# Prompt tokens in even-first order in a two-layer decoder step: dilated attention groups computed among tokens of one parity

## The chip, the cores and the metric

The kernel runs on one core of one Trainium2 chip. The metric is the time of one execution in microseconds of the device (us). Everything is computed in one launch.

## The reference, cut to what matters

Two layers process 256 prompt tokens and 8 x 4 sampled tokens together (model width 1024). The input projection w_in gives queries, keys and values for 12 heads of 64, in three groups of 4 heads, and two gate parts. A prompt query in group g looks at the keys at distances 0, d, 2d, ... up to its window:

```python
DIL_PATTERNS = ((128, 1), (512, 4), (2048, 16))     # (window, dilation) of the groups
dist = dilation * jnp.arange(window // dilation + 1)
...
idx = rows[:, None] - dist[None, :]
valid = idx >= 0
kg = jnp.take(k_all, idx, axis=1)
s = jnp.einsum('bqhd,bqjhd->bqhj', qc, kg).astype(jnp.float32) * scale
s = jnp.where(valid[None, :, None, :], s, NEG)
m = jnp.max(s, -1, keepdims=True)
pr = jnp.exp(s - m)
o = jnp.einsum('bqhj,bqjhd->bqhd', pr, vg.astype(jnp.float32)) / den[..., None]
...
mixw = jax.nn.softmax(jnp.stack(lses, 0), axis=0)   # over the three groups
```

Since the groups are weighted by their denominators, one softmax over the keys of all three groups gives the same. In groups 1 and 2 the distances are multiples of 4 and of 16, so an even query never meets an odd key. The sampled tokens attend to caches of 128, 512 and 1024 positions and to their own few new rows. Beside the attention a gate multiplies u with a causal 128 x 128 product of normalised gate rows (the spatial weights). Then follow the mixer's output projection, a cross attention to 256 memory tokens, and a feed-forward part, each with a residual and a normalisation. Outputs are also the new keys and values.

## The kernel before, in words

Activations lie with features on the partitions and the 288 tokens as columns. A linear layer is done for 128 outputs at a time: for each of 8 k-tiles three matmuls (high part by high weight, low by high, high by low, L361 to L363) of 288 columns. SP loads weights in blocks of 256 columns (`wraw`, three buffers, L148); ACT and DVE split each block half by half into a high part `wh` (L343) and a low part `wl` (L344).

The attention of a layer lies inside and behind the projection w_in, which has 22 blocks of 128 outputs, 528 matmuls. `Tasks` (L170) is a planner: every piece of attention work is a generator that yields costs; while w_in is written out, pieces whose time has come are put between its matmuls, by priority, and what is left is written out behind it (`drain`). Then a scheduler orders each engine's list by a model of the times. On the chip each engine takes its list in order. The pieces are:

- `prompt_all` and `prompt_scores(p)`, p = 0, 1 (L891): for each group g and each half h2 of a pair of heads, scores in a PSUM bank `tr` (three buffers), L902 (128 later queries by 256 keys) and L906 (128 earlier queries by 128 keys), on 64 rows of the array; DVE adds the mask and takes the maximum (L910, custom instruction and a read of the accumulator); exp on ACT (L919); normalisation on DVE (L929); transposes on PE (L933, L935), copied to `pt` by ACT (L939).
- `prompt_pv(p)` (L943): value products L952 and L955, evicted by ACT (L957) and DVE (L958). These are only possible behind w_in, since their targets `attH`, `attL` are set up there.
- `decode_scores`: the caches' keys come in blocks `cu` (128 x 1024, five buffers, and three lent ones, `cv`), are multiplied with the queries on POOL (L1059) or DVE (L1061), and are summed up on DVE (L1062). `query(g)` turns a group's queries by PE (L1041), ACT copies them (L1043), and they go out to DRAM (L1045) and come back spread over the partitions (L1048 on SP's queue). The sums times a constant give `zs` (L1068), which PE adds up (L1074). After the softmax PE transposes the weights `dp` (L1096 to L1109).
- `decode_pv` (L1117): value products of the caches, L1128, 4 matmuls on 32 columns of the array for each block; then the new rows (L1138), a copy (L1141, L1142), transposes (L1149) and copies `at` (L1158, L1160). A cache block's buffer is free when its products are done; only then SP loads the next block into it. The last blocks are group 2's: two halves of 64 partitions for each buffer.
- `natural` (L798): keys and values turned to token order for the outputs (L804, L811); `gate_norm`, `spatial_weights` (L748) and `sgu` (L865; L872, L877): the gate.

SP's list holds all the loads in one order, so a load that waits for a buffer holds up every load behind it. Behind the attention SP also loads the memory's tokens, `mem_nat` (L1195).

## Time and profile before

| what | value |
|---|---|
| three runs | 1072.79, 1073.74, 1076.74 us, median 1073.74 |
| profiled execution | 1073.84 us, its span 1072.1 us |
| PE busy | 1026.8 us, 96% of the span |
| DVE, ACT, POOL busy | 763.2 (71%), 531.0 (50%), 189.2 us (18%) |
| DMA | 213.68 MB, 199 GB/s on average |

The profile shows one execution; its 1.7 us outside the span are start and end of the program. The stages are read from the trace: attention of layer 0 to about 142 us, then mixer, cross attention and feed-forward to 560, attention of layer 1 to 672, and the rest. Busy times of engines overlap. A PE row's length holds the time that a matmul takes through the array; matmuls follow one another faster than that, so the step from one start to the next is the cost.

### The profile page before, as it was taken

How to read it: one execution, taken by the hardware profiler on the slowest of the kernel's cores; microseconds unless marked ns; L12 is line 12 of the kernel's file. 1: busy time of each engine (PE TensorE's matmuls, PEld its weight loads, DVE VectorE, ACT ScalarE, POOL GpSimd, SP SyncE). 2: the span in 40 equal slices, each digit the busy share in tenths (PEclk: the TensorE clock that was granted, in tenths of full speed). 3: DMA queues.
4: the chain of work that ended last, by engine and by line, in shares of the span. 5: the costliest groups of instructions: out<-in, count | busy, mean ns of one | idle time of the engine just before them, and what ended most of it. 6: DMA issues, size and time to landing. Idle time of an engine off the chain costs nothing. (4 is left out here: it accounts for less than half of the span.)

```text
span 1072.1 us, 20130 instructions
## 1 busy us (share of the span) xinstructions
PE 1026.8 (96%) x8038; PEld 958.7 (89%) x8038; DVE 763.2 (71%) x1406; ACT 531.0 (50%) x1000; POOL 189.2 (18%) x151
## 2 busy tenths in 40 slices
PE   8999999999999999999988999999999999999995
PEld 7989589988799999999977985998888999999994
DVE  6698679855489756565996876897464996565656
ACT  4427546543458535353562364565353685354431
POOL 5592013000023000000448500220000410000000
PEclk8999999999999999999999999999999999999997
DMA  9999844777944555544455898447874465545431
GB/s 290 299 260 316 243 166 154 245 267 255 325 129 143 190 169 181 158 158 161 155 162 165 241 302 235 141 161 237 285 277 157 142 177 165 185 163 191 165 117 44
DMA packets 185533, 213.68 MB, mean 199 GB/s; under 512 B 5760, under 2 KB 175136, under 8 KB 185440
## 3 DMA queue, kind: packets, MB, share of 16 engines
q1 hardware_dynamic: 177216, 205.00, 60.1%
q10 hardware_dynamic: 8224, 7.41, 2.1%
q8 instruction: 63, 1.03, 0.4%
q14 instruction: 30, 0.25, 0.1%
HBM read 203.80 MB, written 8.59 MB: 198 GB/s over the span
## 5 line engine op out<-in xcount | busy, mean ns | idle before, releaser
L343 ACT ACTIVATE wh<-wraw 128x1024 fp32r<-128x1024 f32 (+1 forms) x237 | 249.3, 1054 | 285.6 <-PE acc L362 234.2
L344 DVE TENSOR_TENSOR wl<-wraw,wh 128x1024 fp32r<-128x1024 f32 (+1 forms) x237 | 308.4, 1304 | 100.1 <-ACT wh L343 99.5
L361 PE MATMUL acc<-xH,wh 128*128 128x288 f32 x728 | 219.0, 301 | 3.2 <-DVE fy L533 3.2
L363 PE MATMUL acc<-xH,wl 128*128 128x288 f32 x728 | 217.3, 299 | 2.7 <-DVE wl L344 2.7
L362 PE MATMUL acc<-xL,wh 128*128 128x288 f32 x728 | 218.5, 301 | 1.2 <-DVE xL L640 1.2
L361 PE MATMUL acc<-hH,wh 128*128 128x288 f32 x512 | 151.1, 295 | 0.0
L362 PE MATMUL acc<-hL,wh 128*128 128x288 f32 x512 | 151.1, 295 | 0.0
L363 PE MATMUL acc<-hH,wl 128*128 128x288 f32 x512 | 150.8, 295 | 0.0
L361 PEld LDWEIGHTS acc<-xH,wh 128*128 128x128 f32 x728 | 139.5, 192 | 4.4 <-issue 2.5
L363 PEld LDWEIGHTS acc<-xH,wl 128*128 128x128 f32 x728 | 138.9, 191 | 4.0 <-DVE wl L344 3.6
L362 PEld LDWEIGHTS acc<-xL,wh 128*128 128x128 f32 x728 | 139.1, 191 | 2.3 <-DVE xL L640 1.9
L551 POOL TENSOR_TENSOR s<-s,xres 128x288 f32<-128x288 f32 x15 | 20.2, 1349 | 444.8 <-DVE s L547 444.1
L361 PEld LDWEIGHTS acc<-hH,wh 128*128 128x128 f32 x512 | 96.4, 188 | 0.0
L362 PEld LDWEIGHTS acc<-hL,wh 128*128 128x128 f32 x512 | 96.4, 188 | 0.0
L363 PEld LDWEIGHTS acc<-hH,wl 128*128 128x128 f32 x512 | 96.2, 188 | 0.0
L361 PE MATMUL acc<-fH,wh 128*128 128x290 f32 x256 | 78.3, 306 | 1.8 <-DVE fy L533 1.8
L362 PE MATMUL acc<-fL,wh 128*128 128x290 f32 x256 | 76.9, 301 | 0.2 <-DVE fL L525 0.2
L363 PE MATMUL acc<-fH,wl 128*128 128x290 f32 x256 | 75.8, 299 | 0.5 <-DVE wl L344 0.5
L361 PEld LDWEIGHTS acc<-fH,wh 128*128 128x128 f32 x256 | 48.3, 189 | 2.6 <-PE acc L363 2.2
L362 PEld LDWEIGHTS acc<-fL,wh 128*128 128x128 f32 x256 | 48.5, 190 | 1.2 <-DVE fL L525 0.6
L363 PEld LDWEIGHTS acc<-fH,wl 128*128 128x128 f32 x256 | 48.1, 189 | 1.2 <-DVE wl L344 1.0
L1059 POOL TENSOR_TENSOR cu<-cu,qb 128x1024 f32<-128x1024 f32 x15 | 43.5, 2917 | 13.1 <-DMA qb<-qd 9.6
(326 smaller groups left out, 2182.2 us busy)
## 6 DMA issues: line engine op xcount, KB each, us to landing
cu<-cache_mem_kv SPq DMA_DIRECT2D x64, 512.0 KB, 7.4
wraw<-w_up SPq DMA_DIRECT2D x32, 1024.0 KB, 5.5
wraw<-w_down SPq DMA_DIRECT2D x32, 1024.0 KB, 4.8
wraw<-w_in SPq DMA_DIRECT2D x21, 1024.0 KB, 5.7
cu<-cache_kv_w SPq DMA_DIRECT2D x42, 512.0 KB, 8.5
wraw<-w_xkv SPq DMA_DIRECT2D x16, 1024.0 KB, 6.4
wraw<-w_mix_out SPq DMA_DIRECT2D x8, 1024.0 KB, 10.1
wraw<-w_xq SPq DMA_DIRECT2D x8, 1024.0 KB, 4.9
```

The lines of the kernel that those rows point to most:

```text
L343: S.activation(h[:, r], raw[:, r], AF.Copy)
L344: gates[f"split{k}"] = behind(V.tensor_sub(lo[:, r], raw[:, r], h[:, r].bitcast(F32)), "dve")
L361: m = T.matmul(ps, wh[:, k], H[:, k], start=first, stop=False)
L362: T.matmul(ps, wh[:, k], L[:, k], start=False, stop=False)
L363: T.matmul(ps, wl[:, k], H[:, k], start=False, stop=last)
L551: eng.tensor_add(self.s, self.s, xres[:, n])
L1059: G.tensor_mul(cu, cu, qb[g])
```

## The change

The 256 prompt tokens lie in another order: in each half of 128, first the 64 even ones, then the 64 odd ones. The order is made where the tokens are read (a load of two neighbouring tokens to a partition, and transposes that write to the two places); rotary tables, masks, the gate's spatial weights and all outputs are adapted to it (three more output DMAs on ACT's queue in a layer). Group 0 is computed as before. In groups 1 and 2 the scores are taken only among tokens of one parity, on 64 x 64 pieces of the array: the half of rows is h2, the half of columns is the parity h. Their two results share one bank and one set of columns (gg = 1), so masks, exp, normalisation and transposes run over 768 columns for each half instead of 1152. The value products of groups 1 and 2 take 64 columns each. The planner's costs are the same 700 for a step of scores (two steps for each p now, not three), 700 instead of 1000 for a half's transposes, and 650 for each group's value products. Lines move: L902/L906 are L935 (both) for group 0, and L946, L949, L953 for the others; L933/L935 become L982; L952/L955 become L997/L1000 and L1011; L1041 becomes L1098, L1061 L1118, L1062 L1119, L1068 L1125, L1074 L1131, L1096 L1153, L1109 L1166, L1128 L1185, L148 L156, L344 L352, L361 to L363 L369 to L371, L1195 L1252.

```diff
-    dist = 128 + np.arange(128)[:, None] - np.arange(256)[None, :]
-    for g, (win, dil) in enumerate(((128, 1), (512, 4), (2048, 16))):
+    row = np.arange(128)
+    tok = 2 * (row % 64) + row // 64
+    dist = 128 + tok[:, None] - np.concatenate([tok, 128 + tok])[None, :]
+    c[:, C_MQ:C_MQ + 256] = np.where((dist >= 0) & (dist <= 128), 0.0, NEG)
+    for g, (win, dil) in ((1, (512, 4)), (2, (2048, 16))):
+        jj, b = row // 64, row % 64
+        j = jj if g == 1 else 1 - jj
+        key = (128 * j + 2 * b)[None, :] + (row // 64)[:, None]
+        dist = 128 + tok[:, None] - key
         ok = (dist >= 0) & (dist <= win) & (dist % dil == 0)
-        c[:, C_MQ + 256 * g:C_MQ + 256 * (g + 1)] = np.where(ok, 0.0, NEG)
+        c[:, C_MQ + 128 + 128 * g:C_MQ + 256 + 128 * g] = np.where(ok, 0.0, NEG)
...
-        nc.sync.dma_start(out=x_nat[:, :, h], in_=I["x_prompt"][0, :, h].rearrange("(a p) d -> p a d", p=128))
+        nc.sync.dma_start(out=x_nat[:, :, h], in_=I["x_prompt"][0, :, h].rearrange("(p a) d -> p a d", p=128))
...
-            T.transpose(ps[:, 128 * a:128 * a + 128], x_nat[:, a, 128 * n:128 * n + 128], ident)
+            T.transpose(ps[:, 0:256].rearrange("p (j q b) -> p q j b", j=2, q=2)[:, a],
+                        x_nat[:, a, 128 * n:128 * n + 128], ident)
...
-            G.affine_select(out=wm, in_=wm, pattern=[[0, 4], [-1, 128]], compare_op=ALU.is_ge,
-                            fill=0.0, base=0, channel_multiplier=1)
+            wsp = stg("wsp")
+            for q in range(2):
+                G.affine_select(out=wsp.rearrange("p (g q b) -> p q g b", g=4, q=2)[:, q],
+                                in_=wm.rearrange("p g (b q) -> p q g b", q=2)[:, q],
+                                pattern=[[0, 4], [-2, 64]], compare_op=ALU.is_ge, fill=0.0, base=-q,
+                                channel_multiplier=1)
...
-                S.copy(vt[g, a], ps)
+                if g:
+                    src = ps[:, 0:256].rearrange("p (j h c) -> p h j c", j=2, h=2)
+                    S.copy(vt[g, a][:, 0:256].rearrange("p (h j c) -> p h j c", h=2, j=2),
+                           src if g == 1 else src[:, :, ::-1])
+                    S.copy(vt[g, a][:, 256:288], ps[:, 256:288])
+                else:
+                    S.copy(vt[g, a], ps)
...
         def prompt_scores(p):
-            pt = slot([128, 2, 3, 384], name="pt")
+            pt = slot([128, 2, 2, 384], name="pt")
             att[f"pt{p}"] = pt
             sc, ms = [], []
             for h2 in range(2):
-                sc.append(ptile(1152).rearrange("p (g k) -> p g k", g=3))
+                sc.append(ptile(1152)[:, 0:768])
                 ms.append(small(12, "m"))
-            for g in range(3):
+            for gg in range(2):
                 b = [tr(), tr()]
+                if gg == 0:
+                    for q, c, d in (((128, 256), (0, 256), (0, 256)), ((0, 128), (0, 128), (256, 384))):
+                        for h2 in range(2):
+                            r = slice(64 * h2, 64 * h2 + 64)
+                            T.matmul(b[h2][:, d[0]:d[1]], qT[r, p, q[0]:q[1]], kT[r, p, c[0]:c[1]],
+                                     start=True, stop=True)
+                else:
+                    for g in (1, 2):
+                        n = 2 * g + p
+                        for i in (1, 0):
+                            for h2 in range(2):
+                                for h in range(2):
+                                    r, o = slice(64 * h2, 64 * h2 + 64), slice(64 * h, 64 * h + 64)
+                                    keys = kT[r, n, 0:256].rearrange("p (j c) -> p j c", j=2)[:, :, o]
+                                    if i == 0:
+                                        T.matmul(b[h2][o, 192 + 64 * g:256 + 64 * g], qT[r, n, o], keys[:, 0],
+                                                 start=True, stop=True, skip_group_check=True)
+                                    elif g == 1:
+                                        T.matmul(b[h2][o, 0:128], qT[r, n, 128 + 64 * h:192 + 64 * h], keys,
+                                                 start=True, stop=True, skip_group_check=True)
+                                    else:
+                                        for j in range(2):
+                                            T.matmul(b[h2][o, 192 - 64 * j:256 - 64 * j],
+                                                     qT[r, n, 128 + 64 * h:192 + 64 * h], keys[:, j],
+                                                     start=True, stop=True, skip_group_check=True)
                 for h2 in range(2):
-                    r = slice(64 * h2, 64 * h2 + 64)
-                    T.matmul(b[h2][:, 0:256], qT[r, 2 * g + p, 128:256], kT[r, 2 * g + p, 0:256],
-                             start=True, stop=True)
-                for h2 in range(2):
-                    r = slice(64 * h2, 64 * h2 + 64)
-                    T.matmul(b[h2][:, 256:384], qT[r, 2 * g + p, 0:128], kT[r, 2 * g + p, 0:128],
-                             start=True, stop=True)
-                for h2 in range(2):
-                    for i, (k0, k1, c) in enumerate(((0, 256, 0), (256, 384, 128))):
-                        V.tensor_tensor_reduce(out=sc[h2][:, g, k0:k1], in0=b[h2][:, k0:k1], in1=mq[:, g, c:256],
-                                               scale=1.0, scalar=-3e38, op0=ALU.add, op1=ALU.max,
-                                               accum_out=ms[h2][:, 3 * i + g:3 * i + g + 1])
+                    for i, (k0, k1) in enumerate(((0, 256), (256, 384))):
+                        d = 512 * i + (128, 256)[1 - i] * gg
+                        c = (256 * gg, (128, 320)[gg])[i]
+                        V.tensor_tensor_reduce(out=sc[h2][:, d:d + k1 - k0], in0=b[h2][:, k0:k1],
+                                               in1=mq[:, c:c + k1 - k0], scale=1.0, scalar=-3e38,
+                                               op0=ALU.add, op1=ALU.max,
+                                               accum_out=ms[h2][:, 2 * i + gg:2 * i + gg + 1])
...
-                for g in range(3):
+                for gg in range(2):
                     ps = tr()
-                    T.transpose(ps[:, 0:128], s[:, g, 256:384], ident)
-                    for k in range(2):
-                        T.transpose(ps[:, 128 + 128 * k:256 + 128 * k], s[:, g, 128 * k:128 * k + 128], ident)
-                    if g in PT_DVE:
-                        V.tensor_copy(pt[:, h2, g], ps[:, 0:384])
-                    else:
-                        S.copy(pt[:, h2, g], ps[:, 0:384])
-                yield 1000, 0
+                    for n, c in enumerate(((512, 0, 128), (640, 256, 384))[gg]):
+                        T.transpose(ps[:, 128 * n:128 * n + 128], s[:, c:c + 128], ident)
+                    S.copy(pt[:, h2, gg], ps[:, 0:384])
+                yield 700, 0
...
         def prompt_pv(p):
             H, L, pt = att["H"], att["L"], att.pop(f"pt{p}")
-            for g in range(3):
-                ps = acc()
-                for tt in range(2):
-                    for h2 in range(2):
-                        c = 256 * g + 64 * (2 * p + h2)
-                        o = ps[64 * h2:64 * h2 + 64]
-                        if tt == 0:
-                            T.matmul(o[:, 0:256], vn[:, c:c + 64], pt[:, h2, g, 0:256],
-                                     start=True, stop=False, skip_group_check=True)
-                        else:
-                            T.matmul(o[:, 128:256], vn[:, 768 + c:768 + c + 64], pt[:, h2, g, 256:384],
-                                     start=False, stop=True, skip_group_check=True)
-                S.activation(H[:, 2 * g + p, 0:256], ps[:, 0:256], AF.Copy)
-                V.tensor_sub(L[:, 2 * g + p, 0:256], ps[:, 0:256], H[:, 2 * g + p, 0:256].bitcast(F32))
-                yield 650, 0
+            for gs in ((0,), (1, 2)):
+                ps = {g: acc() for g in gs}
+                if 0 in ps:
+                    for tt in range(2):
+                        for h2 in range(2):
+                            c = 64 * (2 * p + h2)
+                            o = ps[0][64 * h2:64 * h2 + 64]
+                            if tt == 0:
+                                T.matmul(o[:, 0:256], vn[:, c:c + 64], pt[:, h2, 0, 0:256],
+                                         start=True, stop=False, skip_group_check=True)
+                            else:
+                                T.matmul(o[:, 128:256], vn[:, 768 + c:768 + c + 64], pt[:, h2, 0, 256:384],
+                                         start=False, stop=True, skip_group_check=True)
+                else:
+                    for i in (1, 0):
+                        for h in range(2):
+                            for g in gs:
+                                for h2 in range(2):
+                                    c = 768 * h + 256 * g + 64 * (2 * p + h2)
+                                    o = ps[g][64 * h2:64 * h2 + 64, 128 * i + 64 * h:128 * i + 64 * h + 64]
+                                    r = slice(0, 128) if i else slice(64 * g - 64, 64 * g)
+                                    k0 = 128 * g * i + 64 * h
+                                    T.matmul(o, vn[r, c:c + 64], pt[r, h2, 1, k0:k0 + 64],
+                                             start=True, stop=True, skip_group_check=True)
+                for g in gs:
+                    S.activation(H[:, 2 * g + p, 0:256], ps[g][:, 0:256], AF.Copy)
+                    V.tensor_sub(L[:, 2 * g + p, 0:256], ps[g][:, 0:256], H[:, 2 * g + p, 0:256].bitcast(F32))
+                yield 650 * len(gs), 0
```

PE in layer 0, where w_in ends. Before: its last matmul (L363), then scores of p = 1, the transposes of the sampled tokens' weights `dp`, value products, and the first cache products (`o<-cu`).

```order
L363 MATMUL acc<-xH,wl 128x288
L902 MATMUL tr<-kT,qT 128x256
L906 MATMUL tr<-kT,qT 128x128
L1096 MATMUL tr<-const,dp 128x128 x2
L1097 MATMUL tr<-const,s_1192 128x128
L1109 MATMUL tr<-const,dp 32x128 x3
L952 MATMUL acc<-pt,vn 64x256 x2
L955 MATMUL acc<-pt,vn 64x128 x2
L902 MATMUL tr<-kT,qT 128x256
L906 MATMUL tr<-kT,qT 128x128
L1128 MATMUL o_1287<-cu,z_87 32x256 x8
L1128 MATMUL o_1287<-cu,zp_89 32x256 x4
```

Now the last scores of p = 1 and the first `dp` transposes stand 34 matmuls of w_in ahead of its end:

```order
L370 MATMUL acc<-xL,wh 128x288
L949 MATMUL tr<-kT,qT 64x128 x2
L946 MATMUL tr<-kT,qT 64x64 x2
L953 MATMUL tr<-kT,qT 64x64 x2
L949 MATMUL tr<-kT,qT 64x128 x2
L946 MATMUL tr<-kT,qT 64x64 x2
L953 MATMUL tr<-kT,qT 64x64 x6
L946 MATMUL tr<-kT,qT 64x64 x4
L1153 MATMUL tr<-const,dp 128x128 x2
L1154 MATMUL tr<-const,s_1229 128x128
L371 MATMUL acc<-xH,wl 128x288
```

And at w_in's end (L371 is its last matmul) the second cache products follow at once; the first four stand nine matmuls ahead of them:

```order
L371 MATMUL acc<-xH,wl 128x288
L1185 MATMUL o_1357<-cu,z_87 32x256 x4
L997 MATMUL acc<-pt,vn 64x256 x2
L1000 MATMUL acc<-pt,vn 64x128 x2
L1185 MATMUL o_1357<-cu,zp_89 32x256 x8
L1185 MATMUL o_1357<-cv,zp_89 32x256 x12
```

No scores are left behind w_in. In the same way the scale products L1131 stand earlier in w_in: 8 of them with 144 of its matmuls still to come in layer 0 (before 116; in layer 1 144 both times), and the next 4 with 87 to come in layer 1 (before 44). Layer 1's transposes of group 2's query (L1098) stand later: 146 to come, before 207.

DVE in layer 1, ahead of group 2's `zs`. Before, its products (L1061) and reduces (L1062) stand between splits of weights:

```order
L344 TENSOR_TENSOR wl<-wraw,wh 128x1024
L1062 TENSOR_REDUCE st<-cu 128x16 x2
L916 TENSOR_REDUCE m<-m 128x2 x2
L344 TENSOR_TENSOR wl<-wraw,wh 128x1024
L1061 TENSOR_TENSOR cu<-cu,qb 128x1024
L917 TENSOR_SCALAR m<-m 128x2 x2
L1062 TENSOR_REDUCE st<-cu 128x16
L344 TENSOR_TENSOR wl<-wraw,wh 128x1024
L1068 TENSOR_TENSOR zs<-st,const 128x512
```

Now:

```order
L1118 TENSOR_TENSOR cu<-cu,qb 128x1024 x2
L975 RECIPROCAL m<-m 128x2
L1119 TENSOR_REDUCE st<-cu 128x16 x3
L977 TENSOR_SCALAR p_6793<-p_6793,m 128x512
L977 TENSOR_SCALAR p_6793<-p_6793,m 128x256
L1119 TENSOR_REDUCE st<-cu 128x16
L352 TENSOR_TENSOR wl<-wraw,wh 128x1024
L1125 TENSOR_TENSOR zs<-st,const 128x512
```

All four blocks' reduces stand together there, and only the products wait for the query's load.

SP, loads behind w_in of layer 0. Before, the memory tokens come behind the last cache halves and three other loads:

```order
L148 DMA wraw<-w_mix_out 128x8x256 x2
L148 DMA cu<-cache_kv_w 128x4x256 x2
L148 DMA cu<-cache_kv_w 64x4x256 x8
L148 DMA cu<-cache_mem_kv 128x1024 x3
L1195 DMA mem_nat<-mem_prompt 128x2x1024
```

Now they stand ahead of the last two halves:

```order
L156 DMA wraw<-w_mix_out 128x8x256 x2
L156 DMA cu<-cache_kv_w 128x4x256 x2
L156 DMA cu<-cache_kv_w 64x4x256 x6
L1252 DMA mem_nat<-mem_prompt 128x2x1024
L156 DMA cu<-cache_kv_w 64x4x256 x2
```

In layer 1 one load of w_mix_out moves likewise, between the last two whole cache blocks, and the query's load (L1105) stands behind eight cache blocks instead of five.

## Rows read from the trace of the kernel before

**Rows 1.** Busy time by stage: engine busy (x instructions), clock, DMA share, GB/s.

```profile
0.00:142.00 142.00, 134.29 (x1000) 115.74 (x1001) 107.04 (x238) 67.51 (x145) 62.04 (x47) 0.96 0.93 282
...
560.00:672.00 112.00, 102.28 (x795) 85.60 (x794) 84.83 (x207) 52.10 (x118) 41.49 (x26) 0.95 0.78 235
```

**Rows 2.** The same for 60 to 80 us (PE, PEld, DVE, ACT, POOL).

```profile
60.00:80.00 20.00, 17.80 (x114) 16.29 (x113) 18.01 (x32) 5.54 (x12) 20.00 (x10) 0.91 1.05 289
```

**Rows 3.** Groups by line and form: busy, mean ns of one, idle before.

```profile
L910 DVE CUSTOM_DVE_ANT_0 p<-tr,const 128x256 f32<-128x256 f32 x24 | 10.0, 416 | 5.6 <-PE tr L906 5.5
```

**Rows 4.** Timeline of PE, two score segments: start, length, engine, line.

```profile
62.74 0.71 PE L902 MATMUL tr<-kT,qT 64*128 64x256 f32 x4
...
63.60 0.40 PE L363 MATMUL acc<-xH,wl 128*128 128x288 f32 x1
...
109.83 0.70 PE L902 MATMUL tr<-kT,qT 64*128 64x256 f32 x2
...
110.68 0.44 PE L1096 MATMUL tr<-const,dp 128*128 128x128 f32 x2
```

**Rows 5.** Timeline of PE: small gate products, transposes, value products.

```profile
133.24 0.66 PE L872 MATMUL tr<-wst,misc 128*64 128x128 f32 x8
133.83 0.30 PE L877 MATMUL tr<-wbd,misc 32*64 32x32 f32 x4
...
607.08 0.60 PE L804 MATMUL tr<-const,kT 128*128 128x128 f32 x4
...
641.38 0.65 PE L952 MATMUL acc<-pt,vn 128*64 128x256 f32 x4
...
642.08 0.60 PE L952 MATMUL acc<-pt,vn 128*64 128x256 f32 x4
```

**Rows 6.** Timeline, layer 0: last POOL product of group 1, zs, scale products.

```profile
78.68 2.36 POOL L1059 TENSOR_TENSOR cu<-cu,qb 128x1024 f32<-128x1024 f32 x1
...
83.72 2.21 DVE L1068 TENSOR_TENSOR zs<-st,const 128x1024 f32<-128x1024 f32 x1
...
87.41 1.29 PE L1074 MATMUL s<-const,zs 128*128 128x16 f32 x11
```

**Rows 7.** Timeline, layer 1: group 2's query, products, a reduce, zs, scale products.

```profile
596.94 0.39 PE L1041 MATMUL tr<-const,qT 128*32 128x128 f32 x2
...
608.90 5.78 POOL L1059 TENSOR_TENSOR cu<-cu,qb 128x1024 f32<-128x1024 f32 x2 [9.55 <-DMA qb<-qd]
...
620.52 1.21 DVE L1062 TENSOR_REDUCE st<-cu 128x16 f32<-128x1024 f32 x1
...
622.78 0.69 DVE L1068 TENSOR_TENSOR zs<-st,const 128x512 f32<-128x512 f32 x1
...
625.96 0.96 PE L1074 MATMUL s<-const,zs 128*128 128x16 f32 x8
```

**Rows 8.** Timeline of SP and PE: both layers' ends of the attention.

```profile
113.83 12.54 SPq L148 DMA_DIRECT2D cu<-cache_kv_w  x10
...
132.05 0.64 PE L1128 MATMUL o<-cu,z 128*32 128x256 f32 x8
...
141.27 0.41 PE L362 MATMUL acc<-attL,wh 128*128 128x288 f32 x1 [0.18 <-DVE attL L887]
...
647.17 7.84 SPq L148 DMA_DIRECT2D cu<-cache_kv_w  x10
...
665.95 0.64 PE L1128 MATMUL o<-cu,z 128*32 128x256 f32 x8
...
669.04 0.56 PE L361 MATMUL acc<-attH,wh 128*128 128x288 f32 x3
670.88 0.40 PE L362 MATMUL acc<-attL,wh 128*128 128x288 f32 x1 [1.27 <-DVE attL L887]
```

**Rows 9.** Busy time in two stretches; the last two columns are DMA share and GB/s.

```profile
132.00:138.00 6.00, 5.85 (x60) 4.07 (x60) 3.22 (x12) 1.57 (x5) 0.00 (x0) 1.00 1.03 400
...
652.00:662.00 10.00, 8.47 (x67) 3.90 (x60) 5.50 (x21) 4.46 (x16) 0.00 (x0) 1.00 1.14 217
```

49 lines of the change are left out of this document (28 added, 21 removed).

## The prediction

> **What bounds the kernel now.** I read the busy times by stage first. In both attention stages TensorE (PE) works for over 90% of the time, while the other engines have room on the average [rows 1]. So most of the time PE sets the end, and work taken from it counts. But the first attention stage is not of one kind. In its stretch from 60 to 80 us POOL works without a pause, DVE for 18.01 of 20 us, and PE only 17.80, at a granted clock of 0.91, between its levels of 1.2 and 2.4 GHz [rows 2]: there the decode products on POOL and DVE set the pace. And the end of the stage hangs on transfers. The value caches of the decode part can be loaded only when the first products L1128 give buffers free, which SP sees at 113.83 and at 647.17; the last of these products runs at 132.05 and 665.95, and the first linear of the mixer can go on at 141.27 and 670.88 [rows 8]. In that time the half-height pieces of group 2's cache move at 217 GB/s with the DMA engines saturated, where other loads reach 400 GB/s [rows 9]. So a layer's attention ends at the release time of the first cache buffer, plus 18.2 us (18.8 in layer 1), plus at least 4.9 us (665.95 to 670.88). The 9.2 us in layer 0 hold PE work that was still queued behind the last product.
>
> **The change part by part.** The sum is made against the profiled execution, 1073.84 us, which is 0.1 us above the median of 1073.74. The stages between and after the attention issue the same instructions in the same order, so I take nothing from them.
>
> *Prompt scores.* Before, a layer has ten segments: two in which both halves h2 run, 0.86 us from row to row (62.74 to 63.60), and eight with one half, 0.85 us (109.83 to 110.68) [rows 4]. With about 0.1 us of pause ahead of each that is 0.95 each, 9.5 us a layer. That a segment of two halves costs no more than one of one half shows that the 64-row tiles run side by side. After, group 0 keeps its part: one segment of two halves and two of one in layer 0 (2.85 us), and one and two in layer 1 (about 2.65 since the latter two follow each other). Groups 1 and 2 become 20 matmuls, 40 passes of fp32, on 64x64 tiles. No row shows such a tile. The nearest are the 128x64 tiles of L872, which go in pairs, about 0.11 us for a pair of 128 columns ((0.66 - 0.32) / 3), and the 32x64 tiles of L877 with 32 columns, about 0.08 us a pair (0.30 - 0.22) [rows 5]. A pair with 64 columns lies between 0.055 (half of 0.11) and 0.08; I take 0.07. Then 4 pairs of 128 columns and 16 of 64 make 1.56, with the pause 1.65 us for each p. If all four tiles run side by side it is half, 0.8; if each pass stands alone, 3.1. With 0.2 us for two more pauses in layer 0 (its p0 comes in three pieces) the scores cost 6.35 and 5.95 us: -3.15 and -3.55.
>
> The Trainium skill ("TensorEngine Tiling (Array Packing)", Performance Considerations, Instruction Overhead) speaks against this part: a matmul carries about 60 cycles of overhead, and one shouldn't split a dimension that is already small. The trace agrees in kind: a quarter of the columns still costs about 0.08 against 0.11 us [rows 5]. By that rule 64 columns are just about at the floor, and the sum would stay as it is.
>
> *Transposes* fall from 18 to 12 for each p. Four take 0.60 us, of which 0.27 is the last one's length, so 0.11 each [rows 5]: 24 x 0.11 = -2.6 us. *Value products*: a group costs 0.70 us now (641.38 to 642.08) [rows 5]; groups 1 and 2 become 32 passes, 16 pairs x 0.07 = 1.12 against 1.40: -0.3 for each p, -1.1 in all (alone each: +0.8 each). Together PE has 6.7 + 2.6 + 1.1 = 10.4 us less to do; between -14 (four tiles abreast) and about 0 (one at a time).
>
> *DVE and ACT.* DVE loses 16 of 48 mask-and-max passes; a 256-column one takes 0.416 us [rows 3]. That counts only where DVE sets the pace, below. The added small copies of V on ACT, the extra output DMAs, the second affine_select on POOL and the strided adds cost nothing where ACT is busy for half the time [rows 1]; in 60 to 80 us POOL has no room, and a select there delays the products by its length. I take 0.3 us of that into the stall below.
>
> *What the new order does in layer 0.* PE comes to the group 1 scale product (L1074, now L1131) with 144 instead of 116 w_in matmuls still to come. A matmul takes 0.13 us ((0.56 - 0.29) / 2, the row at 669.04 in [rows 8]), so 3.7 us earlier, and p0's scores save 4.75 - 2.8 = 1.95 us ahead of it: 87.4 becomes 81.7. But its input zs comes from the last product on POOL, which ends at 81.04, and from DVE, which ended zs at 85.93 [rows 6]. DVE has less to do ahead of it, so zs may come between 83 and 86: PE waits 1.3 to 4.2 us, I take 2.7. It holds w_in's matmuls, which stand behind it. Ahead of the first release PE then does 1.95 less for p0, 0.65 less for transposes, no group of value products (0.70), but all of p1's scores instead of three segments (3.55 against 2.85: +0.7). The release comes at 113.83 - 2.6 + 2.7 = 113.9. The 1 MB load of mem_nat now goes ahead of the last two cache pieces: at 400 GB/s [rows 9] 2.6 us. Three segments of scores that lay behind the release are gone, so PE has time for what remains, and I take the short end: 113.9 + 18.2 + 2.6 + 4.9 = 139.6, against 141.27: -1.7 us.
>
> *In layer 1.* The query of group 2 is transposed (L1041, now L1098) when 146 instead of 207 matmuls are left: 61 x 0.133 = 8.1 us later, less two segments of scores ahead of it that are gone (1.9), plus one new (0.95): 604.1 instead of 596.94. From there to the products on POOL it took 11.96 us, through a DMA out and one back in, and 14.6 us more to the end of zs [rows 7]; of these the work itself (two products and four reduces of 1.2 us on DVE, beside POOL) needs 7.9. So zs ends between 624.0 and 630.7; I take 624.7 for PE's start on L1131 (4 of them), at the lower end since DVE's list has both products and the reduces in one piece there. PE is there earlier: this step has 87 matmuls left instead of 44, 5.7 us before 625.96, less 2.2 us of scores, plus 1.3 of transposes that now come first: 619.1. So it waits about 5.6 us where it hardly waited. After it come 0.96 + 87 x 0.13 + 3.35 (p1's scores) + 0.8 (the dp transposes) + 0.5 (the first cache products): release at 641.6 instead of 647.17. A 1 MB load of w_mix_out now stands between the caches' loads, 2.6 us. End: 641.6 + 18.8 + 2.6 + 4.9 = 667.9, against 670.88: -3.0 us.
>
> Sum: -4.7 us, **1069.1 us**.
>
> **The rivals.**
> (B) The waits do not come, because zs and the query's way back are as much earlier as PE is. For it: DVE is full before zs [rows 2] and loses work. Against: POOL and the DMAs aren't touched. Releases at 111.2 and 636.0 give 136.9 and 662.3: -4.4 and -8.6, 1060.8 us.
> (C) The 64x64 tiles run one after another. For it: no row shows them together. Against: both halves do run together in L902, and column tiles in L872 [rows 4, 5]. Then 1.5 us more for each p in the scores and 1.1 in the values: layer 0's release at 116.9, end +1.3; layer 1 hides p0 in its wait and loses 1.5, -1.6: about 1073.5 us.
> (D) Slower: PE's wait for layer 1's group 2 scales. If zs takes the 14.6 us that it took before, PE stands from 619 to 631, the release comes at 648.1 and the end at 674.4 (+3.5); with the longest wait in layer 0 (4.2, end at 141.1) -0.2: 1077.1. PE's idle time of 2.20 us (20 less 17.80) in the stretch from 60 to 80 us went with the granted clock of 0.91, 1.8 us lost in 20 [rows 2]; that in both layers makes 1080.7 us. It decides once the wait in layer 1 is over 8 us. For it: the query's DMA now stands behind eight cache loads on SP instead of five. Against: those two loads of buffers wait for reduces that DVE now reaches earlier.
>
> The Trainium skill ("TensorEngine Tiling (Array Packing)", Key Properties) says that different tiles load weights and multiply in parallel; by that (C) falls. The rows of L872 agree for column tiles; no row shows it for four.
>
> **How the numbers follow.** A measurement of this kernel can't tell less than about 0.5%, 5.4 us, from no change: faster is below 1068.4, slower above 1079.1. The forecast has a chance of 0.45, with a range of its own of 1065 to 1073, so less than half of it is faster (0.20) and the rest no change (0.25). B has 0.25, nearly all faster; C 0.14, no change; D 0.16, of which 0.12 slower and 0.04 no change. That makes 0.45, 0.43 and 0.12. The range is 1059.5 to 1079.5: from a little below B, since four tiles abreast would save 3.4 us more, into D.
>
> **What would show it.** In the new profile: the segments of L949, L946 and L953 at 1.6 us each (0.8 or 3.1 otherwise); PE idle ahead of L1131 by 1 to 4 us near 82, and by about 5.6 near 620; SP's first release of a value cache near 113.9 and 641.6 (this one less what layer 0 gained); the last L1185 some 21 us later; the first linear of the mixer in full run near 139.6 and 667.9 (less layer 0's gain). The prediction is wrong if either wait is missing or over 8 us, if the caches' last piece comes no later than 18 us behind the release, or if the middle stages change.

## The result, and the profile after

The changed kernel takes 1120.59 us (median of 6 runs, 1111.83 to 1123.13), the kernel before in the same series 1073.26 (1070.69 to 1076.74): a ratio of 1.0429, 95% interval 1.0389 to 1.047. It is 47 us slower where 1069.1 was forecast with a range up to 1079.5. The profiled execution has a span of 1117.5 us and a mean granted clock of 0.956 (before 1072.1 and 0.984).

The losses are found by setting the n-th matmul of the linear layers before against the n-th after: they are the same matmuls in the same order. Up to 59.5 us both kernels run level. Layer 0's attention ends 13 us later, the middle stages add nothing, layer 1's attention adds 13 more, and the last of these matmuls stands at 1084.51 against 1057.83 (+26.7). From there to the end it takes 33.0 us against 14.3: 18.7 more, in a stretch in which PE has next to nothing to do.

Busy time by stage, in the stretches of [rows 1] (PE, PEld, DVE, ACT, POOL; clock; DMA share; GB/s):

```profile
0.00:142.00 142.00, 126.15 (x1023) 110.31 (x1023) 97.75 (x198) 63.59 (x143) 61.20 (x48) 0.93 0.89 266
560.00:672.00 112.00, 95.40 (x780) 85.80 (x778) 88.70 (x174) 50.05 (x116) 50.13 (x35) 0.89 0.64 202
```

PE lost 8 and 7 us of busy time, and the clock fell from 0.96 and 0.95. These stretches no longer hold the same work, so the same view is taken between the same two matmuls of each attention, and behind the last matmul. Before:

```profile
59.50:149.40 89.90, 85.55 (x665) 71.24 (x663) 70.25 (x176) 44.78 (x106) 27.27 (x12) 0.98 0.88 263
577.50:678.90 101.40, 94.57 (x717) 79.35 (x717) 78.72 (x190) 47.35 (x107) 27.55 (x14) 0.95 0.79 240
1057.80:1072.10 14.30, 1.17 (x9) 0.72 (x7) 10.64 (x22) 2.31 (x7) 2.45 (x3) 0.62 0.23 83
```

After, the last row cut out of the end:

```profile
58.90:162.40 103.50, 87.02 (x732) 73.12 (x730) 68.89 (x163) 41.77 (x106) 28.21 (x13) 0.87 0.76 228
588.60:704.70 116.10, 97.69 (x793) 83.14 (x792) 81.05 (x174) 45.48 (x109) 30.07 (x15) 0.85 0.69 210
1084.50:1117.50 33.00, 1.16 (x9) 0.71 (x7) 10.64 (x22) 2.30 (x7) 2.45 (x3) 0.59 0.12 36
1098.00:1102.00 4.00, 0.00 (x0) 0.00 (x0) 0.00 (x0) 0.00 (x0) 0.00 (x0) 0.50 0.13 51
```

How to read this: length less PE's busy time is PE's idle time: 4.4 and 6.8 us before, 16.5 and 18.4 after. The low clock cost half of PE's busy time in the stretches at 0.50 (in layer 0 after the change 70.2 to 73.6, 83.8 to 94.1 and 141.8 to 155.5 us): 1.7 and 4.7 us before, 10.9 and 14.9 after. So idle time grew by 12.1 and 11.6 us, the clock's share by 9.1 and 10.1, and PE's work at full clock fell by 7.7 and 7.0. The sums, 13.6 and 14.7, are what the stretches grew by. (The ends of PE's rows are modelled, so the work saved is rough; the idle time is not.) Somewhat more work was saved than the predicted 5.2 us a layer, and none of it reached the end.

In the last row no engine computes and the DMA share is 0.13, two sixteenths, at 51 GB/s. The timeline of SP shows whose they are; the output stores before,

```profile
1066.19 1.66 SPq L704 DMA_DIRECT2D out_y_prompt<-z  x3
```

and after:

```profile
1092.87 4.92 SPq L713 DMA_DIRECT2D out_y_prompt<-z  x3
1097.84 4.74 SPq L715 DMA_DIRECT2D out_y_sample<-z  x1
1102.62 0.54 SPq L713 DMA_DIRECT2D out_y_prompt<-z  x1
1103.28 4.89 SPq L715 DMA_DIRECT2D out_y_sample<-z  x1
```

Four stores of 256 KB at 51 GB/s need 20.6 us. Their new access pattern, `(b q) d -> q b d`, has the parity as its outermost dimension, of size 2. The Trainium skill ("DMA: Bandwidth & Descriptors", Rules for kernel authors) says that an outermost dimension smaller than 16 keeps a DMA on at most as many engines; the share of 0.13 agrees. Six stores of prompt keys and values in each layer, 128 KB each on ACT's queue, have the same pattern. (The diff above leaves the lines of these stores out; the experiments show them.)

**The scores** run as the change meant it. Timeline of PE, p0 of layer 0 (start, length, engine, line, operation, tile, shape, count, and in brackets idle time ahead and its releaser):

```profile
63.67 0.43 PE L949 MATMUL tr<-kT,qT 64*64 64x128 f32 x4
63.94 0.28 PE L946 MATMUL tr<-kT,qT 64*64 64x64 f32 x4
...
69.29 0.43 PE L949 MATMUL tr<-kT,qT 64*64 64x128 f32 x4 [1.83 <-DVE m L960]
```

Four passes of 128 columns, two pairs, begin 0.27 us ahead of the next line (63.67 to 63.94), 0.13 a pair where [rows 5] gave 0.11; the single records of 64-column passes stand in pairs every 0.055 to 0.058 us, and all 40 passes of layer 0's p1 (from 112.73 on) take about 1.2 us instead of the 1.56 predicted. The third row, another piece of p0, shows what came with it: PE now waits there for DVE's maxima, 1.83 us.

**Layer 0's scale products** (timeline of PE and DVE; compare [rows 6]):

```profile
84.08 0.59 PE L849 MATMUL tr<-const,kT 128*32 128x128 f32 x2 [2.27 <-DVE m L960]
...
85.54 1.22 DVE L1125 TENSOR_TENSOR zs<-st,const 128x1024 f32<-128x1024 f32 x1
...
85.67 0.40 PE L849 MATMUL tr<-const,vt 128*32 128x128 f32 x1 [0.80 <-DVE m L960]
...
86.81 3.38 PE L1131 MATMUL s<-const,zs 128*128 128x16 f32 x15 [0.74 <-DVE zs L1125]
```

DVE ends zs at 86.8 (85.54 + 1.22) where it ended it at 85.93. PE has less to do ahead of it and waits 3.8 us in three places, of which the first two (3.07 us) end with DVE's maxima (L960) and only the last (0.74) with zs; then the products run in 3.38 us for 15, over 0.2 each, where 11 took 1.29 before. The granted clock says why, here and in two later places:

```profile
84.00:88.00 4.00, 2.39 (x10) 1.65 (x10) 4.00 (x9) 2.29 (x7) 1.96 (x1) 0.50 1.01 310
88.00:92.00 4.00, 4.00 (x20) 3.94 (x20) 3.99 (x7) 2.54 (x8) 3.29 (x2) 0.50 0.72 245
...
148.00:152.00 4.00, 2.30 (x8) 1.55 (x8) 3.61 (x15) 1.25 (x3) 0.00 (x0) 0.50 0.04 14
...
642.00:646.00 4.00, 3.82 (x17) 3.69 (x18) 4.00 (x5) 0.96 (x2) 0.00 (x0) 0.50 0.81 270
646.00:650.00 4.00, 4.00 (x17) 3.64 (x19) 0.03 (x1) 0.28 (x1) 0.00 (x0) 0.50 1.00 324
```

A clock of 0.50 is the 1.2 GHz level. At 88 and at 646 us PE is full again and still runs at half speed.

**Layer 1's group 2 query** (SP, POOL, DVE, PE; compare [rows 7]):

```profile
617.13 0.38 PE L1098 MATMUL tr<-const,qT 128*32 128x128 f32 x2
...
622.76 0.62 SPq L1105 DMA_DIRECT2D qb<-qd  x1
...
633.37 4.57 DVE L1118 TENSOR_TENSOR cu<-cu,qb 128x1024 f32<-128x1024 f32 x2 [7.07 <-DMA qb<-qd]
633.41 3.45 POOL L1116 TENSOR_TENSOR cu<-cu,qb 128x1024 f32<-128x1024 f32 x1 [21.12 <-DMA qb<-qd]
...
641.30 0.73 DVE L977 TENSOR_SCALAR p<-p,m 128x512 f32<-128x512 f32 x2
...
642.18 1.51 PE L982 MATMUL tr<-const,p 128*128 128x128 f32 x6 [4.89 <-DVE p L977]
```

Less the 13.7 us that the layer is late, the query is transposed at 603.4 (predicted 604.1). But SP issues its way back 5.6 us later (3.8 before), with five cache and weight loads issued ahead of it since 613, and it lands some 10.6 us after that (8.2 before): 16.3 us to the products, where [rows 7] have 11.96. DVE, which had waited 0.62 us for it before, stands idle for 7.07 us, then does the products and reduces in one piece, and the normalising of p (L977), which is queued behind them, holds PE's transposes for 4.89 us.

**The tails** (timeline of SP and PE, both layers; compare [rows 8]):

```profile
118.84 7.85 SPq L156 DMA_DIRECT2D cu<-cache_kv_w  x8
126.74 0.60 SPq L1252 DMA_DIRECT2D mem_nat<-mem_prompt  x1
128.81 1.71 SPq L156 DMA_DIRECT2D cu<-cache_kv_w  x2
...
142.57 1.08 PE L1185 MATMUL o<-cu,z 128*32 128x256 f32 x8 [3.14 <-DMA cu<-cache_kv_w]
...
147.81 0.66 PE L1206 MATMUL tr<-const,od 128*128 128x128 f32 x2 [1.39 <-DVE od L1199]
...
151.25 0.61 PE L370 MATMUL acc<-attL,wh 128*128 128x288 f32 x1 [1.08 <-DVE attL L918]
...
662.47 0.55 SPq L156 DMA_DIRECT2D cu<-cache_kv_w  x1
...
686.10 0.62 PE L1185 MATMUL o<-cu,z 128*32 128x256 f32 x2
...
693.20 0.61 PE L370 MATMUL acc<-attL,wh 128*128 128x288 f32 x1 [1.37 <-DVE attL L918]
```

In layer 0 the last product starts 23.7 us after the first release (before 18.2), with the mem_nat load ahead of the last two pieces as predicted. PE has run out of other work by then: it waits for the transfers (6.0 us in this layer, 0.8 before), falls to the lower clock, and does the remaining chain at half speed: 8.7 us from the last product to the mixer's row L370. In layer 1 the last products start 23.6 us after the release (before 18.8), and L370 comes 7.1 us behind them (before 4.9).

### The profile page after: what moved, and what is told of

Read it like the earlier page. It is cut to its first block, busy times and chain, and to the rows that moved or that the text cites. A ratio compares the mean times of both kernels' runs of the same rounds, so it can differ in the third digit from the quotient of the medians.

```text
span 1117.5 us, 20371 instructions
## 1 busy us (share of the span) xinstructions
PE 1031.2 (92%) x8174; PEld 964.3 (86%) x8174; DVE 761.3 (68%) x1374; ACT 526.3 (47%) x1002; POOL 189.5 (17%) x153
## 5 line engine op out<-in xcount | busy, mean ns | idle before, releaser
L352 DVE TENSOR_TENSOR wl<-wraw,wh 128x1024 fp32r<-128x1024 f32 (+1 forms) x237 | 310.8, 1314 | 105.8 <-ACT wh L351 103.3
L369 PE MATMUL acc<-xH,wh 128*128 128x288 f32 x728 | 220.9, 304 | 2.9 <-DVE fy L542 2.8
L371 PE MATMUL acc<-xH,wl 128*128 128x288 f32 x728 | 219.1, 302 | 4.2 <-DVE wl L352 4.2
L370 PE MATMUL acc<-xL,wh 128*128 128x288 f32 x728 | 219.9, 303 | 0.3 <-DVE xL L649 0.3
L369 PE MATMUL acc<-hH,wh 128*128 128x288 f32 x512 | 151.9, 297 | 0.0
L370 PE MATMUL acc<-hL,wh 128*128 128x288 f32 x512 | 151.7, 296 | 0.0
L371 PE MATMUL acc<-hH,wl 128*128 128x288 f32 x512 | 151.0, 295 | 0.0
L371 PEld LDWEIGHTS acc<-xH,wl 128*128 128x128 f32 x728 | 140.4, 193 | 6.3 <-DVE wl L352 5.7
L369 PEld LDWEIGHTS acc<-xH,wh 128*128 128x128 f32 x728 | 140.6, 193 | 4.5 <-issue 2.5
L370 PEld LDWEIGHTS acc<-xL,wh 128*128 128x128 f32 x728 | 140.5, 193 | 1.1 <-DVE xL L649 0.9
L371 PEld LDWEIGHTS acc<-hH,wl 128*128 128x128 f32 x512 | 96.7, 189 | 0.0
L369 PEld LDWEIGHTS acc<-hH,wh 128*128 128x128 f32 x512 | 96.5, 188 | 0.0
L370 PEld LDWEIGHTS acc<-hL,wh 128*128 128x128 f32 x512 | 96.3, 188 | 0.0
L369 PE MATMUL acc<-fH,wh 128*128 128x290 f32 x256 | 78.2, 306 | 1.8 <-DVE fy L542 1.8
L370 PE MATMUL acc<-fL,wh 128*128 128x290 f32 x256 | 77.1, 302 | 0.0
L371 PE MATMUL acc<-fH,wl 128*128 128x290 f32 x256 | 75.9, 300 | 0.6 <-DVE wl L352 0.6
L369 PEld LDWEIGHTS acc<-fH,wh 128*128 128x128 f32 x256 | 48.4, 189 | 2.6 <-PE acc L371 2.3
L370 PEld LDWEIGHTS acc<-fL,wh 128*128 128x128 f32 x256 | 48.5, 189 | 0.9 <-DVE fL L534 0.2
L371 PEld LDWEIGHTS acc<-fH,wl 128*128 128x128 f32 x256 | 48.1, 189 | 1.2 <-DVE wl L352 1.0
```

Source lines behind the costliest of these rows:

```text
L352: gates[f"split{k}"] = behind(V.tensor_sub(lo[:, r], raw[:, r], h[:, r].bitcast(F32)), "dve")
L369: m = T.matmul(ps, wh[:, k], H[:, k], start=first, stop=False)
L370: T.matmul(ps, wh[:, k], L[:, k], start=False, stop=False)
L371: T.matmul(ps, wl[:, k], H[:, k], start=False, stop=last)
```

## The experiments

Two theories stood at the start: the new stores cost the time by their pattern (S), or the new order of the work does, through waits and the clock behind them (O). Later runs test what of the order it is. A third theory, that the new pieces are slow in themselves (P), is answered by the score rows above. Each run has the kernel before beside it, with medians from 1069.21 to 1073.26 us; so edits are compared by what they lie above it, and 2 or 3 us between two edits tell nothing. Only edited lines are shown; "base" is the changed kernel with its stores mended (second run).

**Key and value stores, one DMA for each parity.**
```diff
-nc.scalar.dma_start(out=o[...].rearrange("(b q) h d -> q b (h d)", q=2), in_=dst[:, j])
+for q in range(2):
+    nc.scalar.dma_start(out=o[...].rearrange("(j b q) h d -> q b j (h d)", j=2, q=2)[q],
+                        in_=dst[64 * q:64 * q + 64])
```


> The changed kernel, its prompt-key and prompt-value output DMAs that went out parity by parity with the parity as the outer dimension (two rows of blocks) now issued as one DMA for each parity, with 64 rows outermost. Theory S (shape of the store): such a transfer runs on two DMA engines only and keeps the cache and query loads waiting, which cost the two attention stages some 13 us each: about 1094 us, the DMA share between 630 and 640 us no longer near 0.13 to 0.2, POOL's wait for the query's load in layer 1 back from 23 to about 10 us. Theory O (order): the 26 us come from the new order of PE, DVE and SP with its waits on score banks; then the stores' shape is hidden: 1115 to 1121 us.


Measured 1116.06 us, ratio 1.0389 (1.0353 to 1.0424). That is what O gave. The last matmul came at 1077.91, 6.6 us earlier; the end stretch stayed at 33.3 us.

**The same for y_prompt as well (base).**
```diff
-nc.sync.dma_start(out=O["y_prompt"][...].rearrange("(b q) d -> q b d", q=2), in_=z)
+for q in range(2): nc.sync.dma_start(out=O["y_prompt"][...].rearrange("(b q) d -> q b d", q=2)[q],
+                                     in_=z[64 * q:64 * q + 64])
```


> As the kernel with the key and value stores split by parity, and the four stores of the prompt's result split likewise. Theory S: the stretch behind the last matmul falls from 33 to about 14 us (the stores of 256 KB ran at about 51 GB/s on two engines), so about 1074 us or a few us less. Theory O: 1096 to 1101 us, since only the last stretch gains. A rival for the last stretch (the 1 KB pieces at a stride of two rows are slow in themselves, whatever their number of engines): no gain there, 1094 us.


Measured 1099.66, 1.023 (1.0196 to 1.0265). The end stretch falls to 16.7 us; the attention stretches stay long:

```profile
60.30:160.20 99.90, 85.69 (x731) 73.57 (x730) 67.98 (x160) 42.10 (x106) 27.14 (x12) 0.90 0.79 236
586.60:702.90 116.30, 98.33 (x793) 83.45 (x791) 82.61 (x174) 45.59 (x109) 28.63 (x15) 0.85 0.69 209
1082.20:1098.90 16.70, 1.18 (x9) 0.73 (x7) 10.64 (x22) 2.30 (x7) 2.45 (x3) 0.62 0.30 71
```

So S holds for some 21 us (1120.59 to 1099.66), 16.4 of them at the end. The remaining 26.6 us over the kernel before go to O by elimination: 2.3 of them lie in the end stretch, which is still longer than the 14.3 us of before, and the mended stores were not tried in the kernel before. Its last matmul stands at 1082.23 though its attention has the instructions of the run before (1077.91): single profiles of this order scatter by some us.

**The stores alone, in the kernel before.**
```diff
-nc.sync.dma_start(out=O["y_prompt"][0, 128 * a:128 * a + 128, h], in_=z)
+nc.sync.dma_start(out=O["y_prompt"][0, 128 * a:128 * a + 128, h].rearrange("(b q) d -> q b d", q=2), in_=z)
```
and the key and value stores likewise.


> The kernel before, its order of tokens and its arithmetic untouched, with only the stores of the prompt's result, of the keys, and of group 0's values issued with the parity as the outer dimension, as the changed kernel does; the stored rows are thereby in another order than the reference's. Theory S: slower by 19.5 us at the end and by 10 to 26 us in the two attention stages: 1103 to 1119 us. Theory O: only the end: 1092 to 1094 us.


Measured 1103.04, 1.0267 (1.0235 to 1.0298): 30 us from store patterns alone (the stored rows come out in another order). The last matmul is 8.0 us later, in one profile and with PE's order in layer 1 slightly moved, and the end stretch is that of the changed kernel:

```profile
1065.80:1098.80 33.00, 1.13 (x9) 0.68 (x7) 10.63 (x22) 2.30 (x7) 2.45 (x3) 0.56 0.11 36
```

**The planner's price for PE work, nearer to DVE's time.** Scores 700 to 1400, transposes 700 to 1000:
```diff
-yield 700, 1500
+yield 1400, 1500
```


> The changed kernel with the prompt stores split by parity (the base of this set, 1099.7 us), and the planner told that a step of scores costs 1400 instead of 700 and a half's transposes 1000 instead of 700. By that the query of group 2 in layer 1 is turned with 169 of w_in's matmuls left (base 146), and its scale products stand 64 from the end (base 87); in layer 0 the last scores stand 24 from the end (base 40). Theory O (the 24 us that are left come from PE's waits in the new order and from the low clock behind each of them): the wait of 4.6 us ahead of the transposes in layer 1 and the half clock behind it shrink, 1086 to 1094 us. Theory P (the new PE pieces are slow in themselves, whatever their order): 1097 to 1102 us.


Measured 1107.01, 1.0304 (1.0244 to 1.0365). The wait at L982 grew to 6.1 us: no help.

**The same, with zs due 6000 ns and the normalised scores 5000 ns behind their inputs.**
```diff
-yield 0, 1500
+yield 0, 6000
```


> The same base and costs as v3_cost, but the planner also gives 6000 instead of 1500 between zs and the scale products, and 5000 instead of 1500 between the normalisation and its transposes. The last 4 scale products stand 48 from w_in's end in both layers, the transposes lie between 96 and 24 (base 120 to 82). Theory O: no wait of over 2 us ahead of the transposes and scale products in layer 1, 1082 to 1092 us, though the first cache products come later. Theory P: 1097 to 1102 us.


Measured 1094.92, 1.0187 (1.0132 to 1.0242). The wait at L982 is gone, but layer 0 still loses 13.5 us.

**PE work put back:** the score and value products of groups 1 and 2 twice, and as many transposes as the change saves (three for each half, where the expectation says half of them); by the expectation some 9 us in all.
```diff
-for i in (1, 0):
+for i in (1, 1, 0, 0):
+for n in range(2 - gg): T.transpose(ps[:, 384:512], s[:, 128 * n:128 * n + 128], ident)
```


> The base with the score and value matmuls of groups 1 and 2 each issued twice (the second writes the same result again) and half the saved transposes put back: PE has about 2.2 us more to do for each p, 9 us in all. If PE work is what sets the attention's end: 1107 to 1110 us. Theory O: most of it falls into waits that are there anyway and keeps the clock up, 1096 to 1103 us. Theory P: more than 9 us slower, over 1109 us.


Measured 1100.32, 1.0257 (1.0216 to 1.0299): 0.7 us over base, or 2.2 if each is taken against its own kernel before (28.8 and 26.6 us). Little or nothing of the work put back shows, so the work saved was worth little. The order of the scores moves with this edit too, so the size isn't exact.

**The clock in the tails:** eight more matmuls behind each of the last six cache pieces, 10.8 us of PE work in all.
```diff
+for t in range(8 if 2 * g + i // 3 >= 4 else 0):
+    T.matmul(o2[32 * (t % 4):32 * (t % 4) + 32, 256:512], z[:, c:c + 32], cu[...], start=True, ...)
```


> The base with 8 more matmuls behind each of the last cache blocks of a layer (into columns that nobody reads), about 0.9 us of PE work for each of six blocks, where PE waits for the cache loads. Theory O: the loads set the pace there, so the work itself costs nothing, and without pauses the clock stays at 2.4 GHz through the end of the attention: 1092 to 1098 us. Theory P and any view by which PE sets the pace there: 1104 to 1110 us.


Measured 1097.05, 1.0231 (1.0187 to 1.0275), mean clock 0.977 against 0.965: 10.8 us more work (by the expectation's price), and 25.5 us over the kernel before where base has 26.6, which is no difference. (With `start=True` these products spoil sums that are still needed, so this run serves for its time alone.)

**Group 2's query two steps earlier.**
```diff
-QUERY_2 = 4
+QUERY_2 = 2
```


> The base (changed kernel, prompt stores split by parity, 1099.7 us) with group 2's query asked for behind the third instead of the fifth of group 1's products: it is turned with 195 of w_in's matmuls left in layer 1 (base 146; the kernel before 207) and 288 in layer 0 (base 240). Nothing else is edited. Theory O: the wait of 4.6 us ahead of the transposes in layer 1, which hangs on DVE's normalisation behind the products with that query, goes, and with it some 10 us of half clock: 1086 to 1093 us. Theory P (the new pieces are slow in themselves) or a binding chain on POOL and DVE alone: 1097 to 1102 us.


Measured 1100.55, 1.0287 (1.0255 to 1.032). The wait at L982 is gone; 3.6 us at L1131 and 5.3 us in layer 0 took its place.

**The same, with zs due 9000 and 6000 ns behind its input.**
```diff
-yield 0, 1500
+yield 0, 9000 if g == 1 else 6000
```


> As q2_early, and the planner is told that the scale products come 9000 and 6000 instead of 1500 behind zs. The last scale products stand 45 and 24 matmuls from w_in's end (76 to 96), so no w_in matmul waits long for them, but the first cache products come last. Theory O: the wait of PE for zs and for the transposes goes, while the cache loads start later: 1085 to 1095 us, w_in ending earlier than in q2_early in both layers. Theory P: 1097 to 1102 us.


Measured 1094.64, 1.0217 (1.0178 to 1.0257). Layer 1's mixer starts only 5.8 us late, but a few matmuls further on it is 17.7 us late: the last cache products now come behind that start. The loss moved to the tail.

**PE work added to the kernel before:** the score products of groups 1 and 2 twice and one more transpose for each group and half, some 9 us in all by the expectation.
```diff
-for h2 in range(2):
+for h2 in (0, 1, 0, 1) if g else (0, 1):
```


> The kernel before with the score matmuls of groups 1 and 2 issued twice (same result again) and one more transpose into unread columns for each group and half: PE has 16 more score segments' worth, about 7 us, and 16 transposes, 1.8 us. If PE's work sets the attention's end in the kernel before, as the prediction took it: 1081 to 1083 us. If the products on POOL and DVE and the cache loads set it: 1070 to 1076 us. More than 1086 us would mean that PE's order, which the doubled work shifts too, costs by itself.


Measured 1092.0, 1.0201 (1.0174 to 1.0229): +22.8 us, at a clock of 0.988. That is far more than the work, and over the 1086 us from which on the expectation puts it to the order: the scores moved too, in both layers. So the kernel before doesn't take added work for next to nothing, as the changed one does; but how much of the 22.8 us is PE's work, and how much the order that comes with it, was not separated.

**Idle matmuls in the two scale waits** (14 ahead of layer 0's L1131, 22 ahead of layer 1's first transposes of p).
```diff
+for _ in range(14 if g == 1 and l == 0 else 0): T.matmul(s2[:, 192:320], ident, st, ...)
+for _ in range(22 if l == 1 and ... else 0): T.matmul(ps[:, 384:512], ident, const[:, 0:128], ...)
```


> The base (changed kernel, prompt stores split by parity, 1099.7 us) with idle matmuls put where PE waits: 14 of 128 columns, 3 us, ahead of layer 0's first scale products (they read the sums st, so they start when PE's wait for zs starts), and 22, 4.7 us, ahead of layer 1's first transposes of the probabilities. Their results go to columns that nobody reads. Theory O (PE's waits themselves cost little beyond the low clock that follows them): PE has 7.7 us more to do, yet the clock stays at 2.4 GHz behind both places, 1088 to 1096 us. If the waits set the time by their length, no change: 1097 to 1102 us. If PE's work sets it: 1104 to 1108 us.


Measured 1107.55, 1.0308 (1.0275 to 1.0341). In layer 0 the comparison is clean: up to the scale products PE, DVE and POOL have base's order. Base first, then this run (L1133 is base's L1131):

```profile
86.47 3.60 PE L1131 MATMUL s<-const,zs 128*128 128x16 f32 x16 [2.69 <-DVE zs L1125]
89.00:93.00 4.00, 4.00 (x19) 3.94 (x20) 4.00 (x5) 3.43 (x11) 0.00 (x0) 0.52 0.85 272
...
85.89 1.96 PE L1133 MATMUL s<-const,zs 128*128 128x16 f32 x16 [1.16 <-DVE zs L1126]
87.00:91.00 4.00, 4.00 (x34) 3.98 (x34) 4.00 (x9) 2.89 (x10) 1.05 (x1) 1.00 0.95 305
```

Counted from the same matmul ahead of it, zs ends within 0.3 us of base's time; but the clock behind it stays at 1.00. From there to the 25th matmul of w_in behind the scale products it takes 6.3 us, here and in the next run, where the four runs of this order without filling take 8.8 to 9.2. So the low clock alone costs some 2.5 us at this place. The mixer of layer 0 starts 5.2 us late (base 8.9). Layer 1 lost, with a wait of 8.4 us for p behind the filling. But its order is another one: DVE normalises both halves of p (L977) only from 644.04 us on, behind the products with group 2's query, where base has the first half at 623.04, ahead of them. What the filling does in layer 1 is thus not shown.

**The same, with idle matmuls in the tails too.**
```diff
+for t in range(8 if 2 * g + i // 3 >= 4 else 0):
+    T.matmul(o2[32 * (t % 4):32 * (t % 4) + 32, 256:512], z[:, c:c + 32], cu[...], start=False, ...)
```


> As a6_fill, with 8 idle matmuls behind each of the last cache blocks of a layer too (as in a5_tail, but adding to unread columns, so that nothing else changes). Theory O: 4 us less than a6_fill or better, since the end of the attention keeps its clock too: 1084 to 1093 us. If PE's work sets the pace: 1108 us or more.


Measured 1096.49, 1.0206 (1.0166 to 1.0247): 11 us less than the run before, with more instructions; but DVE has base's order again in layer 1, so the tails are not the only difference. Over the kernel before it is 23.7 us, base 26.6. In its two attention stretches the clock is 0.96 and 0.94 where base has 0.90 and 0.85:

```profile
59.10:154.30 95.20, 87.08 (x856) 75.02 (x854) 68.95 (x160) 41.73 (x106) 27.61 (x12) 0.96 0.85 247
581.00:694.10 113.10, 101.39 (x932) 86.85 (x931) 82.93 (x174) 45.21 (x109) 28.98 (x15) 0.94 0.72 215
```

In these profiles layer 0 is 4.7 us shorter than in base and layer 1 3.2, but this one is of the fastest execution (1092.36 us, 4.1 under the median). Idle matmuls hold the clock up; of the whole time they give back 1 to 3 us (a run above with the tails alone, and this one), which is not clear of the scatter.

**Is the kernel before fragile?** Same work, another order, twice: the planner's prices lowered (467 and 700), and the query a step earlier.
```diff
-yield 700, 1500
+yield 467, 1500
```


> The kernel before with only the planner's costs of a p's score steps and transposes lowered to the sums that the changed kernel has (467 for each of three steps, 700 for a half's transposes); no work differs. Layer 0's order on PE is the same, layer 1's moves by a few rows near w_in's end (the scale products stand 47 instead of 44 from it, the last transposes 4 instead of 24). If the order of the kernel before is a lucky one which any shift loses: 1078 to 1090 us. If small shifts cost nothing: 1069 to 1075 us.


Measured 1076.82, 1.0038 (1.0016 to 1.0061).
```diff
-QUERY_2 = 4
+QUERY_2 = 3
```


> The kernel before with group 2's query asked for behind the fourth instead of the fifth of group 1's products; no work differs. Scores move by up to 30 matmuls of w_in in both layers; the scale products stand 123 and 66 from w_in's end in layer 0 (before 116 and 65) and 104 and 44 in layer 1 (before 144 and 44). If the order alone, with the same work, is worth 10 us or more: 1080 to 1092 us. If not: 1069 to 1076 us.


Measured 1076.91, 1.0039 (1.001 to 1.0069). Both lose 4 us. That any other order costs 25 us is refuted for these two.

**The best pieces together:** the earlier query with later zs, idle matmuls in the tails, and the y stores in turn on SP's and ACT's queues.
```diff
-for q in range(2): nc.sync.dma_start(...)
+for q in range(2): (nc.sync, nc.scalar)[q].dma_start(...)
```


> The best of the pieces together: group 2's query asked for earlier and the planner's later scale products (q2z9, 1094.6 us), the idle matmuls behind the last cache blocks (a7_fill), and the eight stores of the prompt's result dealt to SP's and ACT's queues in turn. Theory O: the last stretch falls from 16.6 to 14.5 us and the clock holds at the attention's end, 1082 to 1090 us, still behind the kernel before (1072.8), since the waits for the query's way back stay. If idle matmuls help only in the order of a6_fill: 1092 to 1098 us.


Measured 1097.4, 1.0239 (1.0204 to 1.0274). The last matmul came at 1078.48, the end 15.1 us later. It is 24.7 us over the kernel before, where the earlier query with later zs alone has 25.4: the idle matmuls gained nothing in this order. The gains don't add up, and no version beat the kernel before.

## Why the prediction was wrong

*"The extra output DMAs ... cost nothing", and "the stages between and after the attention issue the same instructions ..., so I take nothing from them."* This step failed outright. It priced stores by number and bytes and not by their pattern. The row at 1098 us and both store experiments show it: 18.7 us at the end, where nothing covers a store, and some 8 us inside the layers of the kernel before. In the changed kernel mending the inner ones gave 2.3 or 6.6 us at the last matmul.

*The PE sum.* The mechanism was right: 64x64 tiles run abreast, rival C is wrong, and the saving of 5.2 us a layer was 7 to 8 by the bookkeeping above. The conclusion drawn from it was wrong. Putting some 9 us back costs 0.7 to 2.2 us, so PE's work hardly sets the time any more.

*The path.* The release of the caches, the way from it to the last product and the chain behind that were the right terms, and each came out longer than forecast. In layer 0 the release was forecast at 113.9 us and came at 118.84; the way was 20.8 and took 23.7; the chain was 4.9 and took 8.7. In layer 1, less its 13.7 us of lateness, it was 641.6 and came at 648.8; 21.4 against 23.6; 4.9 against 7.1. Each layer is thus 11.6 us later than the sum. The sum took PE's waits for 2.7 and 5.6 us in all ahead of the release, and no slow clock.

*The waits.* Those foreseen came, at the places foreseen or next to them: 3.8 us around L1131 in layer 0 (predicted 2.7, bounds 1.3 to 4.2), though mostly behind DVE's maxima, and 4.89 us in layer 1 (predicted 5.6; its own terms give 619.4 for PE's arrival and so 5.3), though at the transposes L982 rather than the scale product. That the sizes fit is in part luck. Rival B is wrong: neither zs nor the query came earlier. Three things were missing. PE waits for DVE's maxima, in all 4.9 us in layer 0 (the two at L849 and 1.83 at 69.29), where the kernel before has no such wait: it seems that scores done in fewer pieces leave DVE's passes uncovered. The query's way was taken at its old length, 11.96 us, and took 16.3; rival D named the loads ahead of it, but not the size (that they are the reason was not tested by itself), and DVE, with the query's products ahead of the normalising in its list, stood still behind it. The tail had PE work left as its cover in the sum; it was gone.

*The clock.* Rival D charged 1.8 us a layer for it and had the right sign at 1080.7 us, with a chance of 0.16. The rows at 0.50 are several and some last beyond their pause; the bookkeeping gives 9 to 10 us a layer. The Trainium skill ("TensorE: Matmul & The Clock Gate", HAM oscillation) describes the like for a matmul loop that waits for a transfer in every step: the pause throttles, and the next step begins slow. The rows at 84 and 88 us agree (0.50 in both, the second with PE full), and so does the filled wait of layer 0, behind which the clock stayed at 1.00.

What stays open: the 23 to 27 us that remain with mended stores in the better versions. Each remedy removed its own wait and brought another; how much is due to the waits themselves, to the clock behind them or to the tail's later loads could not be separated, since nearly every edit also shifts the order. Only at layer 0's scale products is the clock's part shown, some 2.5 us. Not tried: another order of DVE's list alone, with the normalising of p ahead of the products that wait for the query.

## What to carry to other kernels

Price each changed store by its access pattern, its outermost count first, and look at what still covers it at the end of the program. A pause on PE can cost its length plus slow work behind it, so before counting work saved as time saved, ask what that engine needs next and whether that input comes earlier too. Here it didn't: zs and the query's way back came no earlier, the cache loads came later, and saved work became waiting. And compare the order of every engine before two runs are said to differ by one edit.

## What the runs showed of the hardware

Stores with an outermost count of 2 moved 51 GB/s at a DMA share of 0.13. Pairs of 64-column passes on 64x64 tiles ran every 0.055 to 0.058 us, half of the 0.11 of a 128-column pair in [rows 5]: no floor showed at this size. 28 idle matmul passes in a wait (14 instructions) kept the granted clock at 1.00 behind it, where it was 0.52 without them, and 16 small products then ran in 1.96 us instead of 3.60.
